# Values and gates of a hybrid encoder layer as seven block products, gates through DRAM, output projections with tokens as weights

## The chip, the cores and the metric

The kernel runs on one core of a Trainium2 chip. The metric is the device time of one execution in microseconds (us), the median of several runs; lower is better. The core has a matrix engine (TensorE, PE in the profile), a vector engine (VectorE, DVE), an activation engine (ScalarE, ACT), a general engine (GpSimd, POOL), and a queue engine (SyncE, SP) that here only issues transfers. Each takes its instructions strictly in the order in which they were written out for it.

## The reference, cut to what matters

One layer with 512 tokens and width 1024. Of the combined projection, `da_v` (1024 columns) and `gates` (3 x 1024 columns) are what the change computes differently; `w_da_o`, `w_wa_o`, `w_xa_o` and `w_out` are applied in another orientation.

```python
h = rmsnorm(x, attn_norm_g)
proj = h @ w_in                       # 512 x 1024 times 1024 x 8704
da_q, da_k, da_v, wa_q, wa_k, wa_v, xa_q, gates = split(proj)
o_da = diff_attention(da_q, da_k, da_v, ...)      # branch A, 8 heads, per-head rmsnorm
o_wa = window_attention(wa_q, wa_k, wa_v, ...)    # branch B, 16 heads
o_xa = memory_attention(xa_q, mem projections)    # branch C, 4 heads
gate = sigmoid(gates.reshape(b, s, 3, d))
merged = (gate[:, :, 0] * (o_da @ w_da_o) + gate[:, :, 1] * (o_wa @ w_wa_o)
          + gate[:, :, 2] * (o_xa @ w_xa_o))
x = x + merged @ w_out
out = rmsnorm(x + expert_choice_ffn(rmsnorm(x)))  # 16 experts, each takes its 64 best tokens
```

All is float32. The gate is computed as 0.5 (1 + tanh(z / 2)); the factor 0.5 is applied when `merged` is split.

## The kernel before

**Split products.** A large projection runs in a rounded float32 form. Each operand is split into a high part (an ACT copy) and a low part (a subtraction of the high part from the original), and a product is three matmuls: high by high, high by low, low by high. `split_w` (lines 132 to 141) does that for weights: ACT copies a 128 x 1024 piece (line 137), VectorE subtracts (line 138). The activations `h_hi`, `h_lo` (transposed, [feature, token]) are made once in `norm_t`; `split_out` (143 to 149) is its subtraction.

**Two orientations.** `proj_t` (151) holds 128 weight columns in the array and streams all 512 tokens, so that its output is transposed; the q and k projections, the gates and the branch projections use it. `proj_n` (160) holds 128 tokens and streams 256 weight columns; the values of branch A (line 280) and `w_out` (line 568) use it. The three matmuls are lines 155 to 157 and 170 to 172.

**Stages, in program order.** (1) `norm_t` on x, token block by token block, with the A values behind it: four weight slabs of 256 columns. (2) branch A, eight heads, each with its own q and k projection, scores (337, 338), softmax, transposes (353), product with the values (357); after each odd head a per-head RMS norm (line 367) and transposes into `o_hi`, `o_lo` (373). (3) `gate(0)`, then `project(w_da_o)`. (4) branch B, `gate(1)`, half of `project(w_wa_o)`. (5) the memory norm, the other half, branch C, `gate(2)`, `project(w_xa_o)`. (6) `w_out`, router logits, and the choice of tokens. (7) the experts in pairs: gather, gate and up, down, scatter. Their weights stream through a ring of 2 MB slots; a slot is loaded as soon as its previous user is done.

**What sets the order.** A scheduler writes out each engine's instructions ahead of time. It may move later work into gaps of earlier work if buffers and PSUM banks are free; in branch A the tail of the last heads is mixed with matmuls of `gate(0)` and of `project`. SP's queue loads weights through `slab_tile`, two 2 MB slabs of two 1 MB halves each. `gates` is one SBUF tile of a whole branch, so a branch's gates can only be made after the branch before has used its own.

## Time and profile before

| | us |
|---|---|
| median of 3 runs | 1742.58 |
| lowest and highest | 1742.55, 1744.67 |
| the profiled execution, as timed | 1743.53 |
| its span, first to last instruction | 1741.7 |
| TensorE busy | 1652.7 (95%) |
| VectorE busy | 522.4 (30%) |
| ScalarE busy | 453.4 (26%) |
| GpSimd busy | 182.4 (10%) |

Up to about 802 us the dense layer runs, then 20 us of routing, then the experts to the end. The page's chain of work that ended last is 65% TensorE and 31% DMA: TensorE throughout the dense layer and in the first expert pairs, weight transfers later. A matmul's end is modelled, so that neighbouring matmuls overlap in the list; the pace is read from start to start. A float32 matmul outside the rounded form appears as two.

### The profile page before, as it was taken

How to read it: one execution, taken by the hardware profiler on the slowest of the kernel's cores; microseconds unless marked ns; L12 is line 12 of the kernel's file. 1: busy time of each engine (PE TensorE's matmuls, PEld its weight loads, DVE VectorE, ACT ScalarE, POOL GpSimd, SP SyncE). 2: the span in 40 equal slices, each digit the busy share in tenths (PEclk: the TensorE clock that was granted, in tenths of full speed). 3: DMA queues.
4: the chain of work that ended last, by engine and by line, in shares of the span. 5: the costliest groups of instructions: out<-in, count | busy, mean ns of one | idle time of the engine just before them, and what ended most of it. 6: DMA issues, size and time to landing. Idle time of an engine off the chain costs nothing.

```text
span 1741.7 us, 21106 instructions
## 1 busy us (share of the span) xinstructions
PE 1652.7 (95%) x8749; PEld 1033.7 (59%) x8749; DVE 522.4 (30%) x1057; ACT 453.4 (26%) x937; POOL 182.4 (10%) x165
## 2 busy tenths in 40 slices
PE   8999999999999999999999999899898998988986
PEld 7978888887879988897334343243342432422433
DVE  4387753365426453534001010010100100100103
ACT  4367763266543343331000100001000000000011
POOL 2043420045422000100000000000000000000000
PEclk9999999999999999999999999999999999999999
DMA  7343213430223524375999999999999999999996
GB/s 199 94 88 85 73 49 97 121 96 5 94 74 100 175 65 182 108 290 227 382 427 427 428 426 427 426 427 427 426 425 429 427 426 427 426 427 427 427 425 257
DMA packets 104082, 477.65 MB, mean 274 GB/s; under 512 B 5297, under 2 KB 73185, under 8 KB 76978
## 3 DMA queue, kind: packets, MB, share of 16 engines
q1 hardware_dynamic: 102034, 470.83, 67.6%
q0 software_dynamic: 1952, 5.47, 1.6%
q8 instruction: 69, 1.13, 0.3%
q14 instruction: 27, 0.22, 0.0%
HBM read 468.94 MB, written 2.10 MB: 270 GB/s over the span
## 4 chain that ended last, share of the span: by engine, by line
PE 65%; DMA 31%; DVE 1%; ACT 1%; issue 1%; SPq 0%; DVEq 0%; ACTq 0%
DMA slot<-in_w_exp_down_dram 11%; PE gu L716 11%; PE pj L155 8%; PE pj L157 8%; PE pj L156 8%; DMA slot<-in_w_exp_up_dram 6%; PE y L727 4%; PE tr L749 2%; PE pj L170 2%; PE pj L171 2%; PE tr L734 2%; PE pj L172 2%; DMA slab<-in_w_exp_gate_dram 2%; DMA slot<-in_w_exp_gate_dram 2%; DMA hx<-in_w_exp_down_dram 2%; DMA slab<-in_w_exp_up_dram 2%
## 5 line engine op out<-in xcount | busy, mean ns | idle before, releaser
L716 PE MATMUL gu<-slot,sp 128*64 128x512 f32 x1216 | 274.8, 594 | 17.8 <-DMA slot<-in_w_exp_up_dram 17.8
L716 PEld LDWEIGHTS gu<-slot,sp 128*64 128x64 f32 x1216 | 88.5, 137 | 190.9 <-issue 150.5
L138 DVE TENSOR_TENSOR w<-slab,w 128x1024 fp32r<-128x1024 f32 x111 | 145.5, 1312 | 122.9 <-ACT w L137 122.6
L155 PE MATMUL pj<-h_hi,w 128*128 128x512 f32 x464 | 182.2, 393 | 0.2 <-DVE aks L146 0.2
L157 PE MATMUL pj<-h_hi,w 128*128 128x512 f32 x464 | 182.0, 392 | 0.0
L156 PE MATMUL pj<-h_lo,w 128*128 128x512 f32 x464 | 181.5, 391 | 0.0
L775 DVE SCALAR_TENSOR_TENSOR sp<-gu,rpick,sp 128x512 f32<-128x512 f32 x32 | 23.7, 750 | 446.6 <-PE gu L716 406.1
L137 ACT ACTIVATE w<-slab 128x1024 fp32r<-128x1024 f32 x113 | 119.0, 1054 | 117.2 <-PE pj L157 67.3
L727 PE MATMUL y<-slot,sp 128*64 128x512 f32 x544 | 123.0, 597 | 24.5 <-DMA slot<-in_w_exp_down_dram 24.4
L716 PE MATMUL gu<-slab,sp 128*64 128x512 f32 x416 | 99.7, 594 | 4.5 <-DMA slab<-in_w_exp_up_dram 4.5
L769 ACT ACTIVATE sp<-gu,rpick 128x512 f32<-128x512 f32 x32 | 21.7, 687 | 299.6 <-PE gu L716 299.6
L727 PEld LDWEIGHTS y<-slot,sp 128*64 128x64 f32 x544 | 37.6, 136 | 103.9 <-issue 71.8
L155 PEld LDWEIGHTS pj<-h_hi,w 128*128 128x128 f32 x464 | 87.2, 188 | 17.9 <-PE tr L373 0.4
L157 PEld LDWEIGHTS pj<-h_hi,w 128*128 128x128 f32 x464 | 87.1, 188 | 17.5 <-issue 0.2
L156 PEld LDWEIGHTS pj<-h_lo,w 128*128 128x128 f32 x464 | 87.2, 188 | 17.1 <-issue 0.2
L700 POOL TENSOR_TENSOR sp<-sp,aff 128x512 f32<-128x512 f32 x8 | 8.4, 1048 | 772.9 <-PE tr L782 744.7
L779 ACT ACTIVATE sp<-tr 128x512 f32<-128x512 f32 x32 | 17.8, 595 | 271.8 <-PE tr L778 271.8
L731 DVE COPY etmp<-y 128x512 f32<-128x512 f32 x8 | 5.5, 692 | 264.4 <-PE y L727 249.2
L441 POOL TENSOR_SCALAR bpt<-bpt,bst 128x256 f32<-128x256 f32 (+1 forms) x64 | 71.9, 1142 | 93.3 <-DVE bst L437 44.5
L716 PEld LDWEIGHTS gu<-slab,sp 128*64 128x64 f32 x416 | 34.3, 137 | 60.2 <-issue 48.3
L155 PE MATMUL pj<-o_hi,w 128*128 128x512 f32 x168 | 65.3, 392 | 0.9 <-ACT o_hi L145 0.7
L156 PE MATMUL pj<-o_lo,w 128*128 128x512 f32 x168 | 65.6, 392 | 0.0
(320 smaller groups left out, 2731.5 us busy)
## 6 DMA issues: line engine op xcount, KB each, us to landing
slot<-in_w_exp_gate_dram SPq DMA_DIRECT2D x38, 2048.0 KB, 34.3
slot<-in_w_exp_up_dram SPq DMA_DIRECT2D x38, 2048.0 KB, 33.8
slot<-in_w_exp_down_dram SPq DMA_DIRECT2D x34, 2048.0 KB, 34.4
slab<-in_w_exp_gate_dram SPq DMA_DIRECT2D x13, 2048.0 KB, 34.3
slab<-in_w_exp_up_dram SPq DMA_DIRECT2D x13, 2048.0 KB, 33.1
slab<-in_w_in_dram SPq DMA_DIRECT2D x25, 1024.0 KB, 7.7
slab<-in_w_exp_down_dram SPq DMA_DIRECT2D x10, 2048.0 KB, 34.3
hx<-in_w_exp_up_dram SPq DMA_DIRECT2D x6, 2048.0 KB, 34.3
```

The source lines that it names most:

```text
L137: ACT.activation(wh, v, AF.Copy)
L138: lo = (low or DVE).tensor_sub(wl, v, f32(wh))
L155: PE.matmul(ps, wh[:, k, :], ah[:, k, :], start=(k == 0), stop=False)
L156: PE.matmul(ps, wh[:, k, :], al[:, k, :], start=False, stop=False)
L157: PE.matmul(ps, wl[:, k, :], ah[:, k, :], start=False, stop=(k == KT - 1))
L170: PE.matmul(o, ah[:, k, a], wh[:, k % 4, :], start=(k == 0 and first), stop=False, skip_group_check=True)
L171: PE.matmul(o, ah[:, k, a], wl[:, k % 4, :], start=False, stop=False, skip_group_check=True)
L172: PE.matmul(o, al[:, k, a], wh[:, k % 4, :], start=False, stop=(k == KT - 1 and last), skip_group_check=True)
L441: POOL.tensor_scalar(pts[t][:, :n], pts[t][:, :n], st[:, 3, t:t + 1], None, op0=OP.mult)
L716: mm = PE.matmul(ps[fc][i * 64:(i + 1) * 64], xT[:, k, i * 64:(i + 1) * 64], sl[i][:, fc * 512:(fc + 1) * 512], start=(k == 0), stop=(k == ...
L727: PE.matmul(y[i * 64:(i + 1) * 64, :w], hT[:, f, i * 64:(i + 1) * 64], sl[i][:, j, n:n + w], start=(f == 0), stop=(f == DE // P - 1))
L734: PE.matmul(ps, gt[:, t * P:(t + 1) * P], ys[:, :w], start=True, stop=True)
```

## The change

The values of branch A and all three gates are computed first, each 512 x 1024 by 1024 x 1024 product as seven products of quarter blocks in place of eight (`seven`). Sums and differences of blocks of `h` are made and split once (`combos`, in the still unused `o_hi` and `o_lo`); sums and differences of weight blocks are made for each of the four products (`combine`, eight pieces of 128 x 1024 each), on VectorE for the values and on GpSimd for the gates. ACT makes a float32 copy `h32` of the transposed `h` for it. A seven has 168 matmuls of 512 columns, twelve for each split weight piece of 128 x 1024.

The gates are written by DMAs on ACT's queue into DRAM scratch and read back when a branch projection needs them, half a branch at a time. `project` now holds tokens in the array and streams 512 weight columns (`proj_512`); `merged` is [token, feature], so 32 transposes stand ahead of `w_out`, and the first half of `w_out` uses `proj_512` too. One projection half occupies four PSUM banks.

```diff
+    def three(ps, ah, al, wh, wl, first, last):
+        PE.matmul(ps, ah, wh, start=first, stop=False, skip_group_check=True)
+        PE.matmul(ps, ah, wl, start=False, stop=False, skip_group_check=True)
+        PE.matmul(ps, al, wh, start=False, stop=last, skip_group_check=True)
+
+    def proj_512(blocks, ah, al, acc):
+
+        for kb, v in enumerate(blocks):
+            for k2 in range(2):
+                wh, wl = split_w(v[:, 2 * k2:2 * k2 + 2, :], 2, 512)
+                for j in range(2):
+                    k = 4 * kb + 2 * k2 + j
+                    for t, o in enumerate(acc):
+                        a = slice(t * P, (t + 1) * P)
+                        three(o, ah[:, k, a], al[:, k, a], wh[:, j, :], wl[:, j, :], k == 0, k == KT - 1)
...
+                    ACT.activation(whole[:, ks, ts], ps, AF.Copy)
...
-    def gate(branch):
...
+    def project(branch, w_o, merged, first=False, ns=range(2)):
+        for n in ns:
+            g = gates[n]
+            nc.sync.dma_start(g, gate_rows[branch][n])
+            blocks = [block_512(w_o, kb * 4 * P * D + n * 512, D, slab_tile()) for kb in range(2)]
+            acc = [ps_pj(), ps_pj(), ps_s(), ps_s()]
+            proj_512(blocks, o_hi, o_lo, acc)
+            for t in range(TT):
+                m = merged[:, t, n * 512:(n + 1) * 512]
                 if first:
...
+                    DVE.scalar_tensor_tensor(g[:, t], g[:, t], 1.0, acc[t], OP.add, OP.mult)
+                    (DVE if branch == 2 and n else POOL).tensor_add(m, m, g[:, t])
...
+            h11, h12, h21, h22 = (quarter(h32, kb, tb) for tb, kb in ((0, 0), (0, 1), (1, 0), (1, 1)))
...
+            DVE.tensor_add(s1, h21, h22)
+            DVE.tensor_sub(s2, s1, h11)
+            split_out(*combos[1], s2)
+            DVE.tensor_sub(h21, h11, h21)
+            split_out(*combos[2], h21)
+            split_out(*combos[0], s1)
+            DVE.tensor_sub(h12, h12, s2)
+            split_out(*combos[3], h12)
...
+            wbufs.extend((tmp.tile([P, 2048], F32R, name="w3"),
+                          gates_half(F32R).rearrange("p t c -> p (t c)")))
...
+            def seven(b, emit, odd, e):
+                b11, b21, b12, b22 = b
...
+                step(acc, a11, b11, True, False)
+                for t in range(2):
+                    ACT.activation(p1[:, t, :], acc[t], AF.Copy)
+                combine(sub, b11, b12, b11, e)
+                combine(sub, t2, b22, b11, e)
+                step(acc, a12, b21, False, True)
...
+                step(acc, combos[1], t2, True, False)
...
+                combine(sub, b12, b22, b12, e)
+                combine(sub, b21, b21, t2, e)
+                step(acc, combos[2], b12, False, False)
...
+                step(acc, a22, b21, False, True)
...
+                step(acc, combos[0], b11, True, False)
...
+                step(acc, combos[3], b22, False, True)
...
+            seven(bs_, values, False, DVE)
+            for br in range(3):
+                seven(quarters(C_GATE + br * D), gate_to(br), br % 2 == 0, POOL)
...
-        gate(0)
-        merged = mpool.tile([P, KT, S], F32, name="merged", tag="merged", bufs=1)
-        project(w_da_o, merged, True, {2: [ap.tile([P, 2, S], F32R, name="aqs", bufs=2) for _ in range(2)]})
+        merged = mpool.tile([P, TT, D], F32, name="merged", tag="merged", bufs=1)
+        project(0, w_da_o, merged, True)
...
+                PE.transpose(ps[:, k, :], merged[:, t, (4 * n + k) * P:(4 * n + k + 1) * P], ident)
```

The order of instructions, at three places. First VectorE in the values, before: the norm of the second token block (rows with `rs_`, `nx`, `h_lo`) is followed by that of the third and fourth, and no weight is split by VectorE until all are done.

```order
L123 TENSOR_SCALAR rs_u<-ssv 128x1
L146 TENSOR_TENSOR h_lo<-tr,h_hi 128x4x128 x2
L124 RECIPROCAL rs_r<-rs_s 128x1
L125 TENSOR_TENSOR rs_t<-rs_r 128x1
L126 TENSOR_TENSOR rs_t<-rs_t,rs_u 128x1
L127 SCALAR_TENSOR_TENSOR rs_r<-rs_t,rs_r 128x1
L146 TENSOR_TENSOR h_lo<-tr,h_hi 128x4x128
L209 SCALAR_TENSOR_TENSOR nx<-nx,rs_r,sc 128x512 x2
L146 TENSOR_TENSOR h_lo<-tr,h_hi 128x4x128 x3
L138 TENSOR_TENSOR w<-slab,w 128x1024 x3
```

Now, from the combination of weight blocks (L334; `t` is t2) to the split of the first sum of `h` blocks (the first `o_lo` row):

```order
L334 TENSOR_TENSOR slabs<-slabs,t_275 128x1024
L155 TENSOR_TENSOR h_lo<-tr,h_hi 128x4x128
L147 TENSOR_TENSOR w<-t_275,w 128x1024
L155 TENSOR_TENSOR h_lo<-tr,h_hi 128x4x128
L334 TENSOR_TENSOR slabs<-slabs,t_275 128x1024
L147 TENSOR_TENSOR w_280<-slabs,w_280 128x1024
L133 TENSOR_TENSOR rs_t<-rs_t,rs_u 128x1
L147 TENSOR_TENSOR w<-t_275,w 128x1024
L147 TENSOR_TENSOR gates<-slabs,gates 128x1024
L134 SCALAR_TENSOR_TENSOR rs_r<-rs_t,rs_r 128x1
L234 SCALAR_TENSOR_TENSOR nx<-nx,rs_r,sc 128x512 x2
L155 TENSOR_TENSOR h_lo<-tr,h_hi 128x4x128 x2
```

The norm of the last token block (L134, L234) now stands behind all eight combinations and four splits, and the sums of `h` behind that norm. TensorE's third product, its first matmuls on `o_hi`, needs those sums; ahead of it TensorE has 48 matmuls of the first two products.

Second, GpSimd in the same stretch, before: two weight subtractions at the start, then small work and transfers of branch A.

```order
L138 TENSOR_TENSOR w<-slab,w 128x1024 x2
L294 IOTA negd 128x896
L287 DMA rows<-in_attn_norm_g_dram 8x128
L287 DMA rows<-in_mem_norm_g_dram 8x128
L287 DMA rows<-in_ffn_norm_g_dram 8x128
```

Now, one gate (the same again for the other two; each piece is half of a weight block):

```order
L334 TENSOR_TENSOR slabs<-slabs 128x1024 x2
L334 TENSOR_TENSOR t_275<-slabs 128x1024
L334 TENSOR_TENSOR slabs<-slabs 128x1024
L334 TENSOR_TENSOR t_275<-slabs 128x1024
L334 TENSOR_TENSOR slabs<-slabs 128x1024
L334 TENSOR_TENSOR slabs<-slabs,t_275 128x1024 x2
```

Eight pieces a gate have come onto GpSimd, where before it had next to nothing while a gate was made.

Third, TensorE at the end of branch A, before: ahead of the last heads' transposes (L373) and behind them stand matmuls of other columns of the first projection.

```order
L155 MATMUL sc<-o_hi,aqs 128x512
L156 MATMUL sc<-o_lo,aqs 128x512
L157 MATMUL sc<-o_hi,aqs 128x512
L155 MATMUL pj<-o_hi,w 128x512
L156 MATMUL pj<-o_lo,w 128x512
L373 MATMUL tr<-ident,onat 128x128 x8
L157 MATMUL pj<-o_hi,w 128x512
L155 MATMUL pj<-o_hi,w 128x512
L156 MATMUL pj<-o_lo,w 128x512
```

Now (L476 is the last product with the values, L492 those transposes):

```order
L476 MATMUL av<-av,aaT 128x128 x4
L170 MATMUL sc<-w,o_hi 128x512
L171 MATMUL sc<-w,o_hi 128x512
L172 MATMUL sc<-w,o_lo 128x512
L170 MATMUL sc<-w,o_hi 128x512
L171 MATMUL sc<-w,o_hi 128x512
L172 MATMUL sc<-w,o_lo 128x512
L492 MATMUL tr<-ident,onat 128x128 x8
L170 MATMUL pj<-w,o_hi 128x512
L171 MATMUL pj<-w,o_hi 128x512
L170 MATMUL pj<-w,o_hi 128x512
```

Six matmuls now stand between the last product and the transposes, and what follows the transposes needs them, since the projection half that is open holds all four banks and lacks only the last two heads.

## Rows read from the trace of the kernel before

**Rows 1.** Windows: length, busy PE PEld DVE ACT POOL (count), clock, DMA share, GB/s.

```profile
0.00:65.40 65.40, 58.51 (x424) 54.34 (x425) 25.29 (x54) 26.86 (x43) 12.79 (x20) 1.00 0.59 165
65.40:285.00 219.60, 218.02 (x1164) 185.32 (x1163) 143.43 (x346) 143.74 (x319) 61.45 (x48) 1.00 0.31 77
350.00:515.00 165.00, 164.03 (x1037) 133.29 (x1036) 75.04 (x231) 95.51 (x254) 71.90 (x64) 1.00 0.21 65
826.00:1067.00 241.00, 240.42 (x1174) 97.05 (x1174) 25.11 (x42) 16.23 (x25) 2.10 (x2) 1.00 0.99 419
```

**Rows 2.** Timeline of PE in `project`, 512 columns: first and last of 28 matmuls.

```profile
299.42 0.39 PE L155 MATMUL pj<-o_hi,w 128*128 128x512 f32 x1
...
305.54 0.39 PE L155 MATMUL pj<-o_hi,w 128*128 128x512 f32 x1
```

**Rows 3.** Timeline of PE in the values, 256 columns: first and last of ten.

```profile
39.82 0.28 PE L172 MATMUL pj<-w,h_lo 128*128 128x256 f32 x1
...
40.90 0.28 PE L172 MATMUL pj<-w,h_lo 128*128 128x256 f32 x1
```

**Rows 4.** The line that stores the A values: ns min/median/max, first and last start.

```profile
L282 ACT ACTIVATE av<-pj x8: 597/597/597, 22.0 to 64.8; 128x512 f32<-128x512 f32 x8
```

**Rows 5.** Timeline of DVE in the norm and first splits: start, duration, engine, line.

```profile
5.99 0.15 DVE L123 TENSOR_SCALAR rs_u<-ssv 128x1 f32<-128x1 f32 x1 [4.96 <-ACT sq L202]
...
7.18 1.41 DVE L209 SCALAR_TENSOR_TENSOR nx<-nx,rs_r,sc 128x512 f32<-128x512 f32 x2
...
17.28 1.28 DVE L146 TENSOR_TENSOR h_lo<-tr,h_hi 128x512 fp32r<-128x512 f32 x2
...
28.36 1.23 DVE L138 TENSOR_TENSOR w<-slab,w 128x1024 fp32r<-128x1024 f32 x1 [2.44 <-ACT w L137]
```

**Rows 6.** Clock and engines after TensorE's short idle time in the routing.

```profile
804.00:806.00 2.00, 0.62 (x4) 0.52 (x4) 1.12 (x8) 1.93 (x5) 0.00 (x0) 0.75 0.78 311
808.00:810.00 2.00, 2.00 (x3) 0.67 (x2) 1.93 (x4) 0.00 (x0) 0.00 (x0) 0.50 0.98 418
812.00:814.00 2.00, 2.00 (x6) 0.82 (x5) 1.90 (x5) 0.00 (x0) 0.00 (x0) 1.00 1.05 451
820.00:822.00 2.00, 2.00 (x16) 1.71 (x16) 0.23 (x1) 0.00 (x0) 0.00 (x0) 1.00 0.00 0
```

**Rows 7.** GpSimd and VectorE subtracting and adding: ns min/median/max, and one meeting.

```profile
L138 POOL TENSOR_TENSOR w<-slab,w x2: 2352/2384/2417, 9.4 to 13.0; 128x1024 fp32r<-128x1024 f32 x2
L251 POOL TENSOR_TENSOR merged<-merged,gates x16: 1281/1293/2374, 518.5 to 748.4; 128x512 f32<-128x512 f32 x16
L138 DVE TENSOR_TENSOR w<-slab,w x111: 1195/1225/2116, 28.4 to 788.5; 128x1024 fp32r<-128x1024 f32 x111
710.33 1.29 POOL L251 TENSOR_TENSOR merged<-merged,gates 128x512 f32<-128x512 f32 x1 [51.36 <-DVE gates L250]
710.59 2.11 DVE L138 TENSOR_TENSOR w<-slab,w 128x1024 fp32r<-128x1024 f32 x1 [0.41 <-ACT w L137]
709.50 0.69 DVE L250 SCALAR_TENSOR_TENSOR gates<-gates,pj 128x512 f32<-128x512 f32 x1 [2.58 <-PE pj L157]
```

**Rows 8.** Page, costliest groups and DMA issues: the ACT copy, a weight slab.

```profile
L137 ACT ACTIVATE w<-slab 128x1024 fp32r<-128x1024 f32 x113 | 119.0, 1054 | 117.2 <-PE pj L157 67.3
...
slab<-in_w_in_dram SPq DMA_DIRECT2D x25, 1024.0 KB, 7.7
```

**Rows 9.** End of branch A: chain of work (start, us, what), then ACT and DVE.

```profile
269.65 1.79 PE av L357 x16
273.84 1.28 ACT L122 ACT_TABLE_LOAD   x1
276.31 1.23 DVE L369 TENSOR_TENSOR onat<-onat,rs_r 128x1024 f32<-128x1024 f32 x1
280.78 0.87 PE tr L373 x8
281.26 1.27 ACT L148 ACTIVATE o_hi<-tr,gT 128x512 fp32r<-128x512 f32 x2 [2.97 <-PE tr L373]
```

More of the change, by code (lines that the diff above doesn't have):

```diff
@@ L81, in ps_o @@
         return psd.tile([P, 512], F32, name="av", bufs=1)
-    halves_left = []
+    slabs = ring.tile([P, N_RING, 2, 2048], F32, name="slabs")
+    halves = [slabs[:, i // 2, i % 2] for i in range(2 * N_RING)]
+    taken = [0]
     def slab_tile():
-        if not halves_left:
-            t = ring.tile([P, 2, 2048], F32, name="slab", bufs=N_RING)
-            halves_left.extend((t[:, 1], t[:, 0]))
-        return halves_left.pop()
+        i = taken[0] % len(halves)
+        taken[0] += 1
+        return halves[i]
     def slab_256(src, off, ncols):
@@ new lines, in trunk_kernel, with block, quarters, first_block @@
+            h32 = tmp.tile([P, KT, S], F32, name="h32")
+            used = [0]
+            def block(src_col, kb, n):
+                i = (0, 1, 2, 3, 2, 1, 0, 3)[used[0] % 8]
+                used[0] += 1
+                return block_512(w_in, src_col + kb * 4 * P * IN_W + n * 512, IN_W, halves[i])
+            def quarters(col):
+                return [block(col, kb, n) for kb, n in ((0, 0), (1, 0), (0, 1), (1, 1))]
+            bs_ = []
+            def first_block(t):
+                if t < 2:
+                    bs_.append(block(C_DAV, t, 0))
@@ new lines, in trunk_kernel, with quarter @@
+            norm_t(x, TT, g_x, h_hi, h_lo, tmp, gb, first_block, h32)
+            bs_ += [block(C_DAV, kb, 1) for kb in range(2)]
+            def quarter(v, kb, tb):
+                return v[:, 4 * kb:4 * kb + 4, tb * 256:tb * 256 + 256]
+            combos = [(o_hi[:, 2 * i:2 * i + 2, :].rearrange("p a (b c) -> p (a b) c", c=256),
+                       o_lo[:, 2 * i:2 * i + 2, :].rearrange("p a (b c) -> p (a b) c", c=256)) for i in range(4)]
+            h11, h12, h21, h22 = (quarter(h32, kb, tb) for tb, kb in ((0, 0), (0, 1), (1, 0), (1, 1)))
@@ new lines, in trunk_kernel, with combine @@
+            split_out(*combos[3], h12)
+            t2 = tmp.tile([P, 4, 512], F32, name="t2")
+            staged = gates_half()
+            p1, u2, u3 = (tmp.tile([P, 2, 512], F32, name=f"part{i}") for i in range(3))
+            wbufs.extend((tmp.tile([P, 2048], F32R, name="w3"),
+                          gates_half(F32R).rearrange("p t c -> p (t c)")))
+            def combine(op, out, a, b, e):
+                for i in range(2):
+                    ks = slice(2 * i, 2 * i + 2)
+                    op(e)(out[:, ks], a[:, ks], b[:, ks])
@@ new lines, in values, with gate_to, emit @@
+            def values(t, n, ps, more):
+                o = av[:, t, n * 512:(n + 1) * 512]
+                if more is None:
+                    ACT.activation(o, ps, AF.Copy)
+                else:
+                    last[:] = [DVE.tensor_add(o, ps, more)]
+            def gate_to(branch):
+                def emit(t, n, ps, more):
+                    o = staged[:, stage[0] % TT, :]
+                    stage[0] += 1
+                    if more is None:
+                        ACT.activation(o, ps, AF.Tanh, scale=0.5)
+                    else:
+                        DVE.tensor_add(o, ps, more)
+                        ACT.activation(o, o, AF.Tanh, scale=0.5)
+                    nc.scalar.dma_start(gate_rows[branch][n, :, t, :], o)
+                return emit
@@ new lines, in trunk_kernel @@
+            last, stage = [], [0]
+            seven(bs_, values, False, DVE)
+            for br in range(3):
+                seven(quarters(C_GATE + br * D), gate_to(br), br % 2 == 0, POOL)
+            del wbufs[2:]
+        gates = [gates_half() for _ in range(2)]
+        ap = pool(as_, "ap", side="right")
+        rows = ap.tile([4 * KT + 1, P], F32, name="rows")
+        lams = ap.tile([P, 4, 64], F32, name="lams")
+        for i, g in enumerate((attn_norm_g, mem_norm_g, ffn_norm_g, final_norm_g)):
+            nc.gpsimd.dma_start(rows[i * KT:(i + 1) * KT], dap(g, 0, (P, KT), (1, P)))
@@ L455, in trunk_kernel @@
             split_out(o_hi[:, hp, :], o_lo[:, hp, :], po)
-        gate(1)
-        project(w_wa_o, merged, False, {2: ks[:2], 3: [ks[2], bp.tile([P, 2, S], F32R, name="bqs", bufs=3)]}, range(2))
+        project(1, w_wa_o, merged, False, range(1))
     with ExitStack() as cs:
```

196 lines of the change are left out of this document (102 added, 94 removed).

## The prediction

> **What bounds the kernel now.** I read the windows by stage first. In the first 65.4 us TensorE is busy 58.5; in branch A it is busy 218.0 of 219.6, in branch B 164.0 of 165.0, both at full clock [rows 1]. The reader is to see that the dense layer is TensorE's own queue, back to back, while VectorE has 143.4 and ScalarE 143.7 of branch A's 219.6: every matmul taken out is time, as long as nothing else comes in its place. In the experts the DMA share is 0.99 at 419 GB/s [rows 1], so they are bound by weights. The two parts don't trade: at 820 to 822 us the DMAs move nothing [rows 6], since every weight slot is full before the experts begin. A shift of the dense layer's end therefore goes to the end one for one, in either direction. I then read paces from start to start: 6.12 us for 27 matmuls of 512 columns is 0.227 us [rows 2], and 1.08 for nine of 256 columns is 0.120 [rows 3].
>
> **TensorE's count.** Values: 384 x 0.120 = 46.1 us become 168 x 0.227 = 38.1, which is -8.0. Gates: 3 x 192 x 0.227 = 130.8 become 3 x 38.1 = 114.4, -16.4. The first half of `w_out`: 192 x 0.120 = 23.0 become 96 x 0.227 = 21.8, -1.2. The 32 new transposes cost 0.87 / 8 = 0.109 each [rows 9], +3.5. The branch projections keep their number and width of matmuls. Sum -22.1 us, if TensorE never waits for more than before. The rest asks where it will.
>
> **Values: +11.** Before, the last value is stored at 64.8 + 0.6 = 65.4 us [rows 4]. Now VectorE's queue has to be worked off before the third product can begin, since that product takes the first sum of `h` blocks, the sums need all four token blocks, and the norm of the last block is queued behind the combinations of weights. From VectorE's first small operation at 5.99 us [rows 5] I count, by the order: four pairs of the norm's scaling at 1.41 (5.6), four chains of five small operations at some 0.16 (3.2), eight `h_lo` at 0.64 to 0.68 (5.4), eight weight splits at 1.23 (9.8), eight combinations taken at the same 1.23 (9.8), two sums and the split of one at 1.23 (3.7) [rows 5]. That is 37.5 us, so 43.5 without a wait. I add 2 us for the first weights (a 1 MB block takes 7.7 us [rows 8]) and 1.5 us for the last token block's way from VectorE over TensorE and ScalarE back: the third product begins at about 47 us. Ahead of it TensorE has 48 matmuls and the transposes of `h`, some 15 us, where before it worked nearly all this time. Behind it stand 120 x 0.227 = 27.2 us. [...] The end is 47 + 27.2 + 2.2 = 76.4, +11.0. Bounds: +5 if sums and combinations overlap better than a strict queue, +16 if they also wait for weights.
>
> **Gates: -7.4.** A gate needs eight combined pieces on GpSimd, at 2.35 to 2.42 us each [rows 7], 18.9 us, and fourteen splits on VectorE at 1.23, 17.2 us. Both would fit beside 38.1 us of matmuls. But in the one meeting of before, VectorE's subtraction, begun 0.26 us after a GpSimd addition of 1.29, takes 2.11 instead of 1.23, about as if it had begun when GpSimd was done, and a GpSimd addition is stretched to 2.37 [rows 7]; the operation that reads PSUM takes its 0.69 [rows 7]. If the two exclude each other throughout, 18.9 + 17.2 = 36.1 of the 38.1 us are used, with no slack for order. The order is also tight: the piece t2 waits for the block b22 (a load of 7.7 us [rows 8]), then come two pieces on GpSimd, a copy of 1.05 on ScalarE [rows 8] and the split, 2 x 2.4 + 1.05 + 1.23 = 7.1 without a queue, and 13 to 14 us of matmuls (60 x 0.227) stand in front of its user. I take 3 us lost for each gate: -16.4 + 9 = -7.4. Bounds: -16.4 (no loss) and +8 (8 us lost each, all that the meetings can cost beyond the slack).
>
> [...]
>
> **Tail of branch A: +6.5.** The last product with the values ends at 269.65 + 1.79 = 271.44; the heads are normalised at 276.31 + 1.23 = 277.54, with a table load of 1.28 in between [rows 9]. These 6.1 us were filled with matmuls of other columns. Now six stand there, 1.4 us, and all behind the transposes needs the two heads: 4.7 us idle, then about 0.7 for the copy to `o_hi` (1.27 for two [rows 9]), and about 1 for the clock as in [rows 6]. Bounds 3 and 9.
>
> **Branch B: +3.** It loses `gate(1)` as filler, 192 x 0.227 = 43.6 us of its 165.0. ScalarE was busy 95.5 [rows 1], of which I put some 10 to that gate's copies and tanh; 86 of 121 is denser than 144 of 220 in A, which TensorE bore with 1.6 us idle. I take 3 us; bounds -3 and +10. Inside A the same look gives 0 to 2, taken as 0.5.
>
> **Halves and `merged`: +5.3.** Every projection half now takes four banks and ends with the gate's product on VectorE. Six such ends can each show one addition of 1.29 [rows 7], 8 us at most; I take 1.5, since other banks feed the scores. At `merged`: -1.2 + 3.5, and 1.5 (about one such addition ahead of the first transposes), +3.8. The scratch's DMAs cost nothing: in A the DMA share is 0.31 [rows 1], and a gate is read a whole branch after it was written. If that cover is gone, it is a load, 7.7 us.
>
> **Sum.** +11.0 - 7.4 + 6.5 + 3.0 + 0.5 + 3.8 + 1.5 = +18.9 against the profiled execution's 1743.5 (its span is 1741.7), 1762.4. The median of the runs lies 0.95 lower: **1761 us**, rounded down.
>
> **Rivals.**
> - *The count rules* (faster). VectorE and GpSimd stay ahead, and of the 37 to 40 us of losses above fewer than 18 occur. It decides at the third product: if it begins by 33 us and a gate takes no more than 39, the values end near 33 + 27.2 + 2.2 = 62.4 (-3.0), the gates give -16.4 + 3 x 0.9 = -13.7, and half of the other terms' +15.3 is left: -9 in all, 1734, between 1724 and 1739. For it: TensorE's share in all stages; against it: 43.5 us of VectorE's queue, which no order makes shorter than its sum unless ScalarE or GpSimd takes part.
> - *The lock rules* (slower still). If VectorE's ten additions from PSUM per gate (6.9 at 0.69 [rows 7]) also queue behind blocked splits, a gate is 36.1 + 6.9 = 43 us, 4.9 over TensorE's, and the 3 us chain comes on top: the gates are at -16.4 + 14.7 + 9 = +7.3, and the time is 1761 + 14.7 = 1776, up to 1795 if B too is at its bound. It decides where subtractions on VectorE have a median near 2 us in the gates. For it: [rows 7]; against it: one meeting only, and gaps in both queues.
> - *Losses and gains cancel* (1739 to 1750). Half of the values' delay is hidden, with the third product at 38 us, and the tail of A costs 3.
>
> **How the numbers follow.** Forecast, 1750 to 1775: 0.58. Lock, above 1775: 0.13. Cancelling: 0.13, of which 0.08 within 0.2% (3.5 us, about what a measurement of this kernel can tell from no change) and 0.05 slower. Count, below 1739: 0.16. So faster 0.16, same 0.08, slower 0.76. The range leaves out the further half of the count's case and of the lock's: 1736 to 1786.
>
> **What would show it.** Right: TensorE idle for some 15 us or more before the third product, which begins near 47 us; the last value near 76; each gate 40 to 42 us long, with VectorE's subtractions near 2 us wherever GpSimd combines; an idle gap of 4 to 6 us ahead of the last transposes of A; the experts as long as before, and as late as the dense layer. Wrong: the third product before 35 us (the queue was not the limit), gates of 38 us (the lock is hidden), B shorter than its matmuls suggest, or experts that begin later and yet end as before (the shift is not passed on).

## The result, and the profile after

The changed kernel takes 1803.82 us (median of four runs, 1802.91 to 1804.43) against 1743.62 for the kernel before: 1.0343 times as long, 95% interval 1.0325 to 1.0361. The forecast was 1761 with a range of 1736 to 1786: the direction was right, the size was not, and the time lies outside the range.

The windows by stage of the kernel after, to be held against [rows 1] (length, busy us of PE, PEld, DVE, ACT and POOL with counts, granted clock, DMA share, GB/s): up to the third product; the rest of the values; the gates and the start of branch A; branch A from its first score to branch B's; all up to the experts; experts.

```profile
0.00:46.10 46.10, 22.74 (x84) 15.81 (x84) 34.95 (x58) 27.24 (x44) 3.28 (x9) 0.86 0.49 161
46.10:79.00 32.90, 31.28 (x121) 24.46 (x122) 22.38 (x22) 10.61 (x11) 3.23 (x2) 0.88 0.25 81
79.00:250.00 171.00, 149.25 (x602) 117.42 (x602) 116.05 (x90) 69.56 (x85) 74.70 (x34) 0.93 0.49 143
250.00:491.00 241.00, 227.48 (x1218) 194.52 (x1219) 149.08 (x356) 140.14 (x312) 60.85 (x50) 0.96 0.30 85
491.00:886.00 395.00, 385.60 (x2394) 325.18 (x2393) 203.24 (x451) 181.35 (x404) 93.71 (x81) 1.00 0.38 136
886.00:1127.00 241.00, 240.42 (x1172) 96.82 (x1171) 24.90 (x41) 16.25 (x25) 2.10 (x2) 1.00 1.00 419
```

Two things are to be seen. TensorE is idle for 23.4 us before the third product, for 21.8 in the gates and for 13.5 in branch A, where it was idle for 1.6 us of 219.6 before [rows 1]. And the granted clock, 1.00 in every stage of [rows 1], is 0.86 to 0.96 in the first four windows: behind the longer gaps TensorE works for some microseconds at a granted clock of 0.50 (46.0 to 52.0 us and 103.2 to 106.0, the windows at the end). (Some expectations below count the two together: their 34 us without work in the gates are about the 21.8 of idle time and 0.07 x 171 = 12.0 of clock.) The experts are what they were: 240.42 busy of 241.00, 419 GB/s.

Four marks in each kernel's trace make the accounts below comparable: the values' last matmul, branch A's first score, branch B's first score, and the last matmul of the router's logits. All times are us.

| kernel | values' end | to A's first score | A's to B's first score | B's first score to logits' end | logits' end to end | median |
|---|---|---|---|---|---|---|
| before | 65.4 | 19.0 | 267.5, a gate in it | 452.9, two gates in it | 937 | 1743.6 |
| after | 78.6 | 171.3, three gates in it | 240.9 | 373.9 | 937 | 1803.8 |

For before the end of the last store [rows 4] stands for the values' end; its last matmul of the values begins 0.9 us earlier, at 64.5, so by one mark for both the values would have 0.9 us more of the loss and the gates 0.9 less. With a gate at 192 x 0.227 = 43.6 us taken off, branch A took 267.5 - 43.6 = 223.9 and the part behind it 452.9 - 87.2 = 365.7. So the change is +13.2 in the values, 171.3 - 19.0 - 130.8 = +21.5 in the gates, +17.0 in branch A, +8.2 behind it, and nothing in the experts: 59.9 together, against 59.7 between the two spans.

### The profile page after: what moved, and what is told of

Read it like the earlier page. It is cut to its first block, busy times and chain, and to the rows that moved or that the text cites. A ratio compares the mean times of both kernels' runs of the same rounds, so it can differ in the third digit from the quotient of the medians.

```text
span 1801.4 us, 20690 instructions
## 1 busy us (share of the span) xinstructions
PE 1655.8 (92%) x8397; PEld 1015.0 (56%) x8397; DVE 625.3 (35%) x1143; ACT 489.0 (27%) x967; POOL 243.3 (14%) x183
## 4 chain that ended last, share of the span: by engine, by line
PE 51%; DMA 34%; DVE 5%; issue 4%; ACT 3%; POOL 2%; SPq 0%; DVEq 0%; ACTq 0%; POOLq 0%
DMA slot<-in_w_exp_down_dram 10%; DMA slot<-in_w_exp_up_dram 8%; PE gu L845 7%; PE y L856 3%; DMA slabs<-in_w_exp_up_dram 3%; PE pj L164 3%; PE pj L165 3%; PE pj L166 3%; PE sc L170 2%; PE sc L171 2%; PE sc L172 2%; PE pj L170 2%; PE tr L878 2%; PE tr L863 2%; DMA slabs<-in_w_exp_gate_dram 2%
## 5 line engine op out<-in xcount | busy, mean ns | idle before, releaser
L845 PE MATMUL gu<-slot,sp 128*64 128x512 f32 x1216 | 274.1, 594 | 21.6 <-DMA slot<-in_w_exp_up_dram 21.4
L147 DVE TENSOR_TENSOR w<-slabs,w 128x1024 fp32r<-128x1024 f32 x120 | 172.7, 1441 | 158.7 <-ACT w L146 154.1
L146 ACT ACTIVATE w<-slabs 128x1024 fp32r<-128x1024 f32 x120 | 126.9, 1058 | 216.6 <-PE sc L172 72.1
L164 PE MATMUL pj<-h_hi,w 128*128 128x512 f32 x272 | 107.6, 395 | 0.9 <-DVE bqs L529 0.7
L166 PE MATMUL pj<-h_hi,w 128*128 128x512 f32 x272 | 106.5, 392 | 0.0
L165 PE MATMUL pj<-h_lo,w 128*128 128x512 f32 x272 | 106.4, 391 | 0.0
L845 PE MATMUL gu<-slabs,sp 128*64 128x512 f32 x416 | 98.9, 594 | 4.4 <-DMA slabs<-in_w_exp_up_dram 4.4
L908 ACT ACTIVATE sp<-tr 128x512 f32<-128x512 f32 x32 | 17.7, 595 | 272.7 <-PE tr L907 272.7
L170 PE MATMUL pj<-w,o_hi 128*128 128x512 f32 x144 | 58.3, 421 | 14.0 <-DVE part L364 9.7
L170 PE MATMUL sc<-w,o_hi 128*128 128x512 f32 x144 | 56.8, 413 | 12.7 <-DVE part L364 6.1
L845 PEld LDWEIGHTS gu<-slabs,sp 128*64 128x64 f32 x416 | 34.8, 137 | 59.6 <-issue 48.0
L863 PE MATMUL tr<-gates 128*128 128x512 f32 (+1 forms) x128 | 60.6, 600 | 2.1 <-ACT gates L860 0.9
L878 PEld LDWEIGHTS tr<-sp,x 128*128 128x128 f32 x512 | 57.8, 192 | 6.8 <-DVE acc L865 5.3
```

The lines of the kernel that those rows point to most:

```text
L146: ACT.activation(wh, v, AF.Copy)
L147: lo = (low or DVE).tensor_sub(wl, v, f32(wh))
L164: PE.matmul(ps, wh[:, k, :], ah[:, k, :], start=(k == 0), stop=False)
L165: PE.matmul(ps, wh[:, k, :], al[:, k, :], start=False, stop=False)
L166: PE.matmul(ps, wl[:, k, :], ah[:, k, :], start=False, stop=(k == KT - 1))
L170: PE.matmul(ps, ah, wh, start=first, stop=False, skip_group_check=True)
```

## The experiments

### Is it the lock between VectorE and GpSimd?

The gates hold the largest error: 152.3 us for what is 114.4 us of matmuls. My theory was the rival of the prediction called "the lock rules". What it looks like in the second half of the first gate is on the timelines of the kernel after (start, us, engine, line; in brackets the idle time before and what ended it), GpSimd, then VectorE, then TensorE:

```profile
83.44 3.36 POOL L334 TENSOR_TENSOR slabs<-slabs 128x1024 f32<-128x1024 f32 x1
86.76 3.37 POOL L334 TENSOR_TENSOR t<-slabs 128x1024 f32<-128x1024 f32 x1
90.08 3.39 POOL L334 TENSOR_TENSOR slabs<-slabs 128x1024 f32<-128x1024 f32 x1
93.43 6.67 POOL L334 TENSOR_TENSOR slabs<-slabs,t 128x1024 f32<-128x1024 f32 x2
119.86 3.47 POOL L334 TENSOR_TENSOR slabs<-slabs 128x1024 f32<-128x1024 f32 x1 [19.76 <-DMA slabs<-in_w_in_dram]
```

```profile
87.80 3.40 DVE L147 TENSOR_TENSOR w<-slabs,w 128x1024 fp32r<-128x1024 f32 x1
91.25 3.30 DVE L147 TENSOR_TENSOR gates<-t,gates 128x1024 fp32r<-128x1024 f32 x1
94.48 8.03 DVE L147 TENSOR_TENSOR w<-slabs,w 128x1024 fp32r<-128x1024 f32 x3
102.42 1.28 DVE L364 TENSOR_TENSOR part<-pj,part 128x512 f32<-128x512 f32 x2
```

```profile
103.25 0.77 PE L170 MATMUL pj<-w,o_hi 128*128 128x512 f32 x1 [6.05 <-DVE part L364]
```

GpSimd's pieces, 2.4 us in [rows 7], take 3.4, and VectorE's splits, 1.23, take up to 3.4, about as if each waited for the other's end: GpSimd's second piece here ends at 86.76 + 3.37 = 90.13, and a split of 1.22 from there would end at 91.35, where VectorE's ends at 87.80 + 3.40 = 91.20; GpSimd's third, 2.4 from 91.20, would end at 93.60 and ends at 90.08 + 3.39 = 93.47. Between 79 and 235 us VectorE's 43 splits take 88.3 us, 35.9 more than 43 x 1.22. TensorE's 6 us of idle time end with an addition that reads an accumulator (L364); that addition is itself not slow, 1.28 for two, but it stands in VectorE's queue behind the slow splits. Two other explanations fit these rows as well: that the chain from block to combination to split is too long whoever makes it, and that TensorE waits because VectorE must read the accumulators between two products. The first two kernels ask this.

**Combinations on VectorE.**

```diff
-                seven(quarters(C_GATE + br * D), gate_to(br), br % 2 == 0, POOL)
+                seven(quarters(C_GATE + br * D), gate_to(br), br % 2 == 0, DVE)
```

> The gates' combinations of weight blocks are made by VectorE, like those of the values; nothing else is changed (after: 1803.8 us, TensorE without work for about 34 us between 85 and 247 us). Theory, the lock: VectorE's splits and GpSimd's combinations exclude each other, and that is what stretches VectorE's queue. Then no split takes more than 1.3 us here, VectorE needs 22 x 1.23 + 6.9 = 34 us of a gate's 38.1, and some 20 to 28 us come back: 1776 to 1784. Rival, the chain: the way from block to combination to split to product is too long whichever engine combines: within 4 us of after, 1800 to 1807. Second rival, VectorE at 34 of 38.1 is the new bound: later than after, above 1808.

Measured: 1780.98 us, 1.0217 (1.0201 to 1.0232) times before, 22.8 less than after. The split line of VectorE between 85 and 235 us (ns min/median/max, first and last start):

```profile
L147 DVE TENSOR_TENSOR w<-slabs,w x32: 1210/1220/1227, 87.0 to 231.5; 128x1024 fp32r<-128x1024 f32 x32
```

No split is longer than 1.23 us. VectorE makes eight more pieces for each gate, and all is sooner. The chain has as many steps as before, but a piece now takes 1.22 us where GpSimd took 2.4 to 3.4, so that this run alone doesn't tell the lock from a chain that is too long with GpSimd in it.

**No combinations.**

```diff
             def combine(op, out, a, b, e):
+                if e is POOL:
+                    return
...
-                step(acc, combos[1], t2, True, False)
+                step(acc, combos[1], b22 if e is POOL else t2, True, False)
```

> The gates' combinations are left out: the products take the weight blocks as loaded (so the gates' values are others), with the same 168 matmuls and 14 splits for each gate, and nothing on GpSimd. Lock: all of the stretching goes, gates of 38 to 40 us, 1771 to 1778. Chain: as much goes, since the combination is part of the chain. Rival, the banks: TensorE waits because VectorE has to read the accumulators between two products that use the same ones; that wait stays and at most 8 us come back: 1795 or more.

Measured: 1771.92 us, 1.0163 (1.0148 to 1.0178), 31.9 less than after. The additions that read accumulators between products are still there, so the banks are not the cause. This is the floor: the combinations cost 9.1 us if VectorE makes them and 31.9 if GpSimd does.

**One operand.** Moving the work also changes how long it takes and in whose queue. So GpSimd kept the combinations, and VectorE's split was made to read less.

```diff
         ACT.activation(wh, v, AF.Copy)
+        if one:
+            DVE.tensor_scalar(wl, f32(wh), 1.0 / 4096.0, None, op0=OP.mult)
+            return wh, wl
...
-                        wh, wl = split_w(v[:, 2 * k2:2 * k2 + 2, :], 2, 512)
+                        wh, wl = split_w(v[:, 2 * k2:2 * k2 + 2, :], 2, 512, one=e is POOL)
```

> In the gates the low part of a weight is made from the high part alone (times 1/4096), so that VectorE's split reads one SBUF operand and not two (the gates' values are others); GpSimd still combines the blocks, and every wait of the chain stands. Theory, the lock by operands: one-operand instructions don't meet GpSimd's; GpSimd's pieces are back at 2.4 us and the gates at 41 to 43 us each, 22 to 28 us less than after's 1803.8: 1776 to 1782. Rival, GpSimd itself: it is slow (2.4 us a piece, 19 us a gate), and a chain through it is long whatever VectorE reads; then GpSimd's pieces may shrink, but TensorE waits as before: 1797 to 1804.

Measured: 1776.61 us, 1.0190 (1.0173 to 1.0207). The time is the one forecast, but the reason given was not right. The two engines between 85 and 235 us:

```profile
L148 DVE TENSOR_SCALAR w<-w x29: 677/695/2885, 83.6 to 192.4; 128x1024 fp32r<-128x1024 f32 x29
L337 POOL TENSOR_TENSOR slabs<-slabs x10: 2407/2825/2908, 85.2 to 167.3; 128x1024 f32<-128x1024 f32 x10
```

The scaling still takes up to 2.89 us instead of 0.69, and GpSimd's pieces a median of 2.83 instead of 2.4. It reads one operand, but 1024 columns in 0.69 us, which is nearly twice the pace of the subtraction. The gain could have come from the shorter instruction alone.

**One operand at the old pace.**

```diff
         ACT.activation(wh, v, AF.Copy)
+        if one:
+            DVE.tensor_reduce(wl, f32(wh)[:, :, :, None], AX.X, OP.add)
+            return wh, wl
```

> As the kernel with one operand, but the low part is made by a reduction over a last dimension of length one, which also reads only the high part (the gates' values are others); the one-operand scaling took 0.69 us for a piece when alone and up to 2.9 beside GpSimd, so it still met GpSimd, only for less time. If what counts is two reads at a time (two operands, or one operand in two halves), the reduction should take about 1.2 us, as the subtraction does, and never more than 1.3 beside GpSimd, and GpSimd's pieces about 2.4 us: then VectorE's work for a gate is that of after, and the time still falls to 1770 to 1778. Rival: what counted was VectorE's shorter work, 0.69 for 1.23; then a reduction of 1.2 us meets GpSimd as the subtraction did, and the time is back at 1795 to 1804.

Measured: 1773.59 us, 1.0171 (1.0157 to 1.0185), 30.2 less than after.

```profile
L149 DVE TENSOR_REDUCE w<-w x28: 1207/1220/1223, 84.5 to 189.4; 128x1024 fp32r<-128x1024 f32 x28
L338 POOL TENSOR_TENSOR slabs<-slabs x10: 2399/2409/2431, 84.5 to 164.4; 128x1024 f32<-128x1024 f32 x10
```

VectorE's instruction takes the 1.22 us of the subtraction, GpSimd does the same pieces, and neither engine's are stretched: the longest of all 38 reductions between 85 and 235 us takes 1.223 us, and the longest of GpSimd's 20 pieces 2.451. From the values' end to branch A's first score it is 142.9 us instead of 171.3. So the lock costs up to 28.4 us, and it goes with the instruction that VectorE runs beside GpSimd's pieces, not with how much work the two have: subtractions of two operands take up to 3.41 us in after, scalings up to 2.89 in the run above, reductions never more than 1.223. Why the three differ was not shown. A chain that is too long with GpSimd in it is out as well, since GpSimd's pieces are all still there at 2.4 us. One wait has changed as well, which both one-operand expectations overlooked: the scaling and the reduction don't read the loaded block, so that GpSimd's pieces and the next loads wait for ScalarE's copy of a block, where in after they waited for VectorE's split of it. One piece of GpSimd in after, then one with the reduction:

```profile
78.18 2.40 POOL L334 TENSOR_TENSOR slabs<-slabs 128x1024 f32<-128x1024 f32 x1 [5.22 <-DVE gates L147]
```

```profile
153.63 2.40 POOL L338 TENSOR_TENSOR slabs<-slabs 128x1024 f32<-128x1024 f32 x1 [3.15 <-ACT gates L146]
```

What part of the 28.4 us this is was not separated. It isn't all: with the combinations on VectorE the splits read the blocks as in after, nothing is held, and 21.4 us of this stretch come back though VectorE makes 24 pieces more.

### The values

**Values by eight.**

```diff
+            def eight(b, emit):
+                b11, b21, b12, b22 = b
+                for n, blocks in enumerate(((b11, b21), (b12, b22))):
+                    acc = [ps_pj(), ps_pj(), ps_s(), ps_s()]
+                    proj_512(blocks, h_hi, h_lo, acc)
+                    for t in range(TT):
+                        emit(t, n, acc[t], None)
...
-            seven(bs_, values, False, DVE)
+            eight(bs_, values)
```

(The sums of the blocks of `h` are moved behind it.)

> The values by eight products with 512 columns (192 matmuls x 0.227 = 43.6 us instead of 38.1), no combination of their weights; the sums of the blocks of h stand behind the values; the gates as in after. The prediction's account: TensorE's lack of work in the values falls from about 35 us to about 13, as in the kernel before, so -22 + 5.4 = -16: 1785 to 1790. Rival: the sums of h and the first gate's combinations meet on VectorE and GpSimd, and the first gate waits for what the values no longer wait for: only 3 to 8 us come back, 1796 to 1801.

Measured: 1777.48 us, 1.0195 (1.0178 to 1.0212), 26.3 less than after. The values' last matmul begins at 60.9 instead of 78.6, which is 17.7 us and close to what was expected. The rest was not: from there to branch A's first score it is 163.9 instead of 171.3, because GpSimd now combines the first gate's blocks while the values run (from 50 us on), and that gate takes 40.4 us from its first matmul to the next gate's instead of 48.9. Its windows, up to the 49th matmul of the values and from there to their end:

```profile
0.00:27.30 27.30, 20.88 (x76) 14.71 (x77) 16.21 (x39) 16.62 (x30) 3.28 (x9) 1.00 0.91 310
27.30:61.00 33.70, 33.70 (x153) 27.72 (x152) 21.25 (x18) 17.45 (x23) 9.66 (x4) 1.00 0.21 64
```

TensorE has no gap from 27.3 us to the values' end, and the clock doesn't fall.

**Both.** Values by eight and the gates' combinations on VectorE, the two edits above together.

> Values by eight products and the gates' combinations on VectorE, both at once. If the two causes are apart from each other, the gains add up: 1803.8 - 26.3 - 22.8 = 1754.7, say 1752 to 1758. If they share VectorE (the first gate's combinations were made by GpSimd while the values ran, and now stand in VectorE's queue behind the sums of h), 4 to 8 us of it are lost: 1759 to 1763.

Measured: 1764.16 us, 1.0116 (1.0101 to 1.0131), 9.5 more than the two gains added, and my reason for that was wrong. From its first matmul to the next gate's, the first gate takes 48.9 us in after, 40.4 with values by eight, 40.4 with combinations on VectorE, and 39.2 with both. VectorE's queue doesn't hold it up; each edit alone had cured it, and adding the gains counted its 8.5 us twice.

**All by eight.** No combinations, 192 matmuls for the values and for each gate.

```diff
-                seven(quarters(C_GATE + br * D), gate_to(br), br % 2 == 0, POOL)
+                eight(quarters(C_GATE + br * D), gate_to(br))
```

> Values and gates by eight products of 512 columns (192 matmuls each, 8 weight splits instead of 14), no combinations at all; order, DRAM scratch and projections as in after. It prices the sevens: TensorE has 4 x 5.4 = 21.8 us more than in after, VectorE 6 splits a gate less. From the values' measured 60.9 us, three gates at 43.6 to 45 and the rest as in after (values' end to A's first score 19, A 240, then 374 to the end of the routing): 1803.8 - 249.9 + 60.9 + 133 + 19 = 1767, within 4. That would be 37 us faster with more matmuls. If sevens with combinations on VectorE are worth their price, the kernel with values by eight and gates by seven on VectorE is faster than this one by 5 to 12 us; if not, this one is the faster.

Measured: 1769.00 us, 1.0143 (1.0127 to 1.0158): 34.8 less than after, with 96 matmuls of 512 columns more. The gates and branch A's start, then the same stage with sevens on VectorE (first of this kernel, then of the kernel with combinations on VectorE alone):

```profile
61.00:213.40 152.40, 152.02 (x667) 124.70 (x666) 38.22 (x41) 46.84 (x60) 1.07 (x2) 1.00 0.47 149
```

```profile
79.00:228.60 149.60, 143.11 (x603) 113.05 (x601) 104.98 (x112) 69.18 (x84) 1.06 (x2) 0.99 0.54 160
```

By the count the sevens take 16.4 us off this stage. They take 8.9 off TensorE's busy time and 2.8 off its length, for 66.8 us more on VectorE. The kernel with values by eight and sevens on VectorE, 1764.16, is 4.8 us faster than this one, just under the 5 to 12 that were to show the sevens worth their price: 2.0 us of it are in this stage (150.8 against 152.8 from the values' last matmul to A's first score), the rest in branch A (239.4 against 243.0).

### Branch A

Branch A is 15 to 19 us longer than before whatever stands ahead of it: 238.8 to 243.0 us in all kernels so far, against 223.9. Most of it sits at the norm of the third and of the fourth pair of heads, here the third pair of after:

```profile
390.38 1.28 ACT L129 ACT_TABLE_LOAD   x1
...
392.85 1.23 DVE L488 TENSOR_TENSOR onat<-onat,rs_r 128x1024 f32<-128x1024 f32 x1
...
394.22 1.94 PE L492 MATMUL tr<-ident,onat 128*128 128x128 f32 x8 [6.89 <-DVE onat L488]
```

It is the chain of [rows 9], but at a place that the prediction had not looked at. Two causes were possible: the open projection half holds four banks, or nothing is left that could stand in the gap.

**The half opened later.**

```diff
+    def three(ps, ah, al, wh, wl, first, last, hold=False):
+        (tc.keep_in_program_order if hold else (lambda i: i))(PE.matmul(ps, ah, wh, start=first, stop=False, skip_group_check=True))
...
-            proj_512(blocks, o_hi, o_lo, acc)
+            proj_512(blocks, o_hi, o_lo, acc, branch == 0 and n == 0)
```

> The first matmul of the first projection half is kept behind branch A's scores in TensorE's order, so that the half takes its four PSUM banks nine scores later than in after. Theory, the banks: the open half holds both banks of the q and k projections and two of the three of the scores, and so the last two heads run thin: the 10.7 us without work at 380 to 400 us mostly go, the tail gets up to 5 us longer: 1795 to 1800. Rival, the norm's chain: the wait is that of each pair's norm (4 squares, table load, small operations), which the half's matmuls partly fill: the gap at 380 stays or grows and the tail grows: 1805 to 1812.

Measured: 1803.49 us, 1.0347 (1.0332 to 1.0363), the same as after. The half now opens behind all scores, where nine of 64 pairs of score matmuls stood behind its opening. Windows of branch A of this kernel:

```profile
370.00:380.00 10.00, 8.94 (x51) 6.14 (x49) 9.49 (x35) 8.93 (x30) 6.97 (x5) 1.00 0.13 26
380.00:392.00 12.00, 4.16 (x18) 3.42 (x19) 8.67 (x21) 6.95 (x19) 5.21 (x4) 0.62 0.00 0
392.00:405.00 13.00, 13.00 (x86) 11.89 (x86) 4.07 (x14) 8.54 (x22) 3.13 (x2) 0.95 0.01 2
405.00:417.00 12.00, 5.77 (x41) 5.52 (x40) 2.62 (x7) 6.04 (x18) 0.00 (x0) 0.86 0.00 0
```

The gaps are still there, 7.8 us of idle time in the second row and 6.2 in the fourth. TensorE's one long gap at the third pair is 7.1 us, 6.9 in after; that at the fourth grows from 3.3 to 6.2. Neither of my two expectations gave "no change" as the answer, but the banks are not the cause: with them free, the third pair's gap stays.

**A gate as filler.**

```diff
-            for br in range(3):
+            for br in range(1, 3):
...
+        for c in range(4):
+            bank, acc = banks(TT, ps_pj)
+            run(proj_n(slab_256(w_in, C_GATE + c * 256, IN_W), h_hi, h_lo, acc))
+            for i, a in enumerate(bank):
+                ACT.activation(gates[c // 2][:, 2 * i:2 * i + 2, c % 2 * 256:c % 2 * 256 + 256], a, AF.Tanh, scale=0.5)
         project(0, w_da_o, merged, True)
```

> As the kernel with values by eight and combinations on VectorE, but the gate of branch A is made behind branch A's heads in program order, by eight products of 256 columns as in the kernel before (384 x 0.120 = 46.1 us, kept in SBUF), so that the scheduler has matmuls again that wait for no head. Theory, the filler: branch A takes some 17 us longer from its first score to branch B's first than before with the gate's matmuls taken off (240.9 against 267.5 - 43.6 = 223.9 us), because nothing is left to fill its gaps; with the filler 12 to 17 us come back, and one gate by seven, about 43 us, is replaced by 46.1: 9 to 14 us less than the kernel without. Rival: the gaps belong to the projection with tokens as weights and its four banks; a filler that needs both banks of the q and k projections doesn't get in, and the time stays or grows by 3 us.

Measured: 1745.56 us, 1.0011 (1.0001 to 1.0020), 18.6 less than without the filler. Branch A from its first score to B's, without and then with it:

```profile
211.80:451.10 239.30, 226.52 (x1220) 192.11 (x1219) 150.51 (x354) 141.41 (x311) 63.61 (x50) 0.97 0.30 85
```

```profile
166.70:433.00 266.30, 264.54 (x1601) 235.19 (x1600) 159.53 (x363) 154.07 (x328) 60.99 (x50) 1.00 0.32 92
```

With 46.1 us more of matmuls the stage is 27.0 us longer, so 19.1 us of them stood where TensorE had waited or run at a lower granted clock (0.97 over the stage without the filler). TensorE's idle time falls from 12.8 to 1.8 us and its clock is 1.00. The projection half opens behind all scores here too, but that alone changed nothing in the run above. This is the cause: the gate was what kept branch A full.

### A version that beats both?

Sevens and scratch left aside, what remains of the change is 512 columns in place of 256. The kernel before with that alone, first for the values:

```diff
-        for s in range(4):
-            sl = slab_256(w_in, C_DAV + s * 256, IN_W) if s else first
-            bank, acc = banks(TT, ps_pj)
-            run(proj_n(sl, h_hi, h_lo, acc, not s, None if s else POOL))
+        for s in range(2):
+            blocks = [block_512(w_in, C_DAV + kb * 4 * P * IN_W + 512, IN_W, slab_tile())
+                      for kb in range(2)] if s else first
+            bank = [ps_pj(), ps_pj(), ps_s(), ps_s()]
+            proj_512(blocks, h_hi, h_lo, bank)
```

> The kernel before, with only its values changed: eight products of 512 columns with tokens as weights, all splits on VectorE. In the kernels with values by eight the values' last matmul begins at 61 us instead of the 65 of before, and what follows is that of before: 1743.6 - 4.3 = 1739, within 1.5. Rival: branch A's first projections, which the scheduler mixed into the values, no longer fit there since the values hold four banks, and what is won goes back: 1742 to 1745.

Measured: 1743.34 us, 0.9997 (0.9988 to 1.0006): nothing that can be measured. The time is in the rival's range, but not for its reason. The values' last matmul begins at 64.2 us, 64.5 before, and not at 61; branch A's first score comes at 83.9 us instead of 84.4, so little was won to be given back, and TensorE is busy for 57.76 of the first 65.4 us where it was 58.51 before [rows 1]:

```profile
0.00:65.40 65.40, 57.76 (x234) 43.57 (x235) 25.15 (x50) 25.32 (x41) 7.97 (x18) 1.00 0.55 164
```

The 61 us of the other kernels came with two more buffers for split weights; whether these make the difference was not tried.

Then the first half of `w_out` as well:

```diff
-    for s in range(4):
-        sl = slab_256(w_out, s * 256, D)
+    for s in range(1, 4):
+        cols = slice(0, 512) if s == 1 else slice(s * 256, (s + 1) * 256)
+        if s == 1:
+            bank = [ps_pj(), ps_pj(), ps_s(), ps_s()]
+            proj_512(blocks, m_hi, m_lo, bank)
```

> The same, and the first half of w_out with 512 columns too: 96 x 0.227 = 21.8 instead of 192 x 0.120 = 23.0, so 1.2 us less than the one before it, about 1738. Rival: the router's logits follow half by half instead of quarter by quarter, and the routing begins as much later: the same or up to 2 us later.

Measured: 1741.81 us, 0.9988 (0.9979 to 0.9997). The logits end at 803.0 us instead of 804.4 in the kernel with the values alone, near the 1.2 us of the count; the 1738 were not reached, since the kernel it builds on had not reached its 1739. It is the fastest kernel here, by 2 us, about what can be told from no change.

## Why the prediction was wrong

- **What bounds the kernel: right.** From the logits' end to the end it is 937.0 us before and 936.7 after; the dense layer's 60 us went to the end one for one.
- **TensorE's count: right, and it decided little.** By eight the gates and branch A's start take 152.4 us, where the count gives 130.8 + 19.0 = 149.8; by seven the count's -16.4 is -2.8 even where GpSimd has no part.
- **Values, +11: nearly right, +13.2.** The third product was put at "about 47 us", and its first matmul starts at 46.16; the queue was read correctly from the order and the durations of [rows 5]. VectorE's rows of after just ahead of it are the last split, the norm of the last block and the first sum; TensorE's are the transposes of that block and the product:

```profile
36.24 1.22 DVE L147 TENSOR_TENSOR gates<-slabs,gates 128x1024 fp32r<-128x1024 f32 x1
37.38 0.15 DVE L134 SCALAR_TENSOR_TENSOR rs_r<-rs_t,rs_r 128x1 f32<-128x1 f32 x1
37.56 1.40 DVE L234 SCALAR_TENSOR_TENSOR nx<-nx,rs_r,sc 128x512 f32<-128x512 f32 x2
...
42.53 1.23 DVE L317 TENSOR_TENSOR nx<-h 128x1024 f32<-128x1024 f32 x1 [0.66 <-ACT h L241]
...
38.57 1.94 PE L238 MATMUL tr<-ident,nx 128*128 128x128 f32 x8 [8.91 <-DVE nx L234]
46.16 0.80 PE L170 MATMUL sc<-w,o_hi 128*128 128x512 f32 x1 [5.65 <-ACT o_hi L154]
```

The 2.2 us that the sum adds to 47 + 27.2 are a term that no run shows; in its place the window from 46.1 to 79.0 us shows TensorE idle for 1.6 of 32.9 us, and a granted 0.88, which over 32.9 us is 3.9.
- **Gates, -7.4: this is the step that failed; they came out at +21.5.** The mechanism was named, but mis-sized: 3 us were taken as lost for each gate, so that the term came out with the wrong sign. "If the two exclude each other throughout, 18.9 + 17.2 = 36.1 of the 38.1 us are used" treats the exclusion as work spread evenly over a gate. It is not: GpSimd waits 19.8 us for its next block, then has most of its pieces together, and VectorE's splits of the same blocks come in the same 20 us. In the window from 84 to 104 us VectorE is busy for 19.80 us, GpSimd for 16.09, and TensorE, whose products need VectorE's additions from behind that queue, only for 13.28:

```profile
84.00:104.00 20.00, 13.28 (x52) 9.54 (x51) 19.80 (x11) 9.82 (x12) 16.09 (x5) 0.94 0.10 28
```

On top comes the clock: 0.93 over the stage's 171 us. The upper bound, 8 us lost for each gate, was worked out from the sum of the meetings and was as wrong: 37.9 / 3 = 12.6 were lost, up to 9.5 of them by the lock. Without the lock, as in the kernel with the reductions, 142.9 - 19.0 - 114.4 = 9.5 us are lost in all three, where the prediction had 9 with it.
- **The rival "the lock rules" had the right mechanism**, with 0.13 of the chances and 1776, up to 1795; the time is beyond that too. It too summed evenly (43 us for a gate, and 3), where a gate takes 50.8, and it left branch A at the forecast's figure. Its sign, a median near 2 us, was badly chosen: the median of the splits of loaded blocks stays at 1.23 and that of GpSimd's pieces goes from 2.4 to 3.4.
- **Tail and interior of branch A, +7: measured +17.0, the second step that failed.** The price of one norm's chain was about right: at the last pair 3.3 us of idle time and 0.29 x 8.1 = 2.3 of clock, 5.7 against 6.5. But I counted it once, at the last pair, and took 0.5 for the rest "by the same look" at the load of ScalarE and VectorE. The third pair has the same chain, 6.9 us and 0.36 x 10.8 = 3.9 of clock. The last pair's row and the windows behind both gaps, in after:

```profile
427.99 1.30 PE L492 MATMUL tr<-ident,onat 128*128 128x128 f32 x5 [3.34 <-DVE onat L488]
...
394.20:405.00 10.80, 10.07 (x50) 8.88 (x50) 5.28 (x15) 6.49 (x12) 1.44 (x1) 0.64 0.01 2
427.90:436.00 8.10, 8.02 (x29) 6.56 (x30) 1.50 (x2) 1.37 (x2) 0.00 (x0) 0.71 0.01 2
```

Before, the same gate had filled both: its tanh stands beside the norm of the third pair, and again at 276.7 us beside that of the fourth.

```profile
231.26 1.23 DVE L369 TENSOR_TENSOR onat<-onat,rs_r 128x1024 f32<-128x1024 f32 x1
231.70 0.60 ACT L233 ACTIVATE gates<-pj 128x512 f32<-128x512 f32 x1
```

- **Branch B, halves and `merged`: +8.3 in the sum, +8.2 measured, in part by luck.** To the end of the last branch projection (747.5 us before, 806.2 after) it is +7.0, where B's 3 and the halves' 1.5 make 4.5; from there to the logits' end it is +1.2, where 3.8 were taken. Ten of the 32 transposes stand ahead of that mark, so that the split is not exact. The scratch's DMAs cost nothing that the trace shows: a gate's read lands 5.9 us after its issue, and nothing waits for it.
- **The other two rivals** ("the count rules", "losses and gains cancel") are out: the third product was at 46 us, and the first gate took 48.9 us. (The losses that the first of them puts at 37 to 40 us add up to 22.1 + 18.9 = 41.0 in the sum.)

By these measures the sum would have been 1743.5 + 13.2 + 21.5 + 17.0 + 8.2 = 1803.4.

## What to carry to other kernels

When work is put on GpSimd to free VectorE, look at which instructions of the two stand in the same microseconds, not at the sum over a stage: here the splits and the combinations of the same blocks came together (from 84 to 104 us VectorE was busy for 19.80 of 20.00 us, GpSimd for 16.09), and subtractions were stretched from 1.22 to as much as 3.41 us where reductions kept their 1.22. Before a stage is moved, ask what else it was good for: a long run of matmuls that waits for nothing is the filler of the stage next to it, and taking it away uncovers each gap that it filled, not the last one alone. Fewer matmuls pay only while the operands are ready: eight products were 35 us faster than seven as the change makes them, and for the gates alone seven with combinations on VectorE were 5 us faster than eight.

## What the runs showed of the hardware

- A VectorE subtraction of 128 x 1024 with two SBUF operands takes 1.22 us, up to 3.41 beside GpSimd's combinations, and these a median of 3.36 instead of 2.41 (after, between 85 and 235 us). A scaling with one operand takes a median of 0.69 and up to 2.89 beside them, and they 2.83. A reduction with one operand takes 1.21 to 1.22 us throughout, and they 2.40 to 2.45.
- In after, TensorE's granted clock is 0.50 from 46.0 to 52.0 us, in the first 6 us of the third product (5.65 us of waiting ahead of it), and 0.50 from 103.2 to 106.0 in the first gate (6.05 us of waiting ahead), where it is 1.00 again from 109.0 to 112.0.

```profile
46.00:52.00 6.00, 4.47 (x10) 3.07 (x11) 5.83 (x6) 2.22 (x3) 0.00 (x0) 0.50 0.00 0
103.20:106.00 2.80, 2.75 (x7) 2.20 (x8) 1.64 (x2) 0.00 (x0) 0.00 (x0) 0.50 0.80 216
109.00:112.00 3.00, 3.00 (x15) 2.46 (x14) 1.22 (x2) 1.68 (x2) 0.00 (x0) 1.00 0.34 130
```

The gaps in the gates thus cost more than their length: TensorE's busy time is 149.25 us with the lock and 143.11 with the combinations on VectorE, for the same matmuls, which is 6.1 us beside the 15.3 us of waits.
